# Low parts of U's chunks by adding DMA, beside the top-k and beside the dense weights

## The chip, the cores and the metric

One core of a Trainium2 chip runs the kernel. The metric is the device time of one execution in microseconds (us), taken as the median of several runs. Engines are named as the profile names them: PE (TensorE), DVE (VectorE), ACT (ScalarE), POOL (GpSimd), SP (SyncE, which only issues DMAs here).

## What is computed

The layer is a decoder block of two sub-layers on 512 tokens of width 1024. The part that the change touches is the second one, a retrieval over 16384 single-neuron experts (`peer_u` and `peer_v`, 16384 x 1024 each), 8 heads, 16 experts per head:

```python
q1, q2 = q[..., :PEER_HALF], q[..., PEER_HALF:]
s1 = jnp.einsum('thd,hkd->thk', q1, sub_k1)
s2 = jnp.einsum('thd,hkd->thk', q2, sub_k2)
v1, i1 = lax.top_k(s1, PEER_TOPK)
v2, i2 = lax.top_k(s2, PEER_TOPK)
cand = (v1[..., :, None] + v2[..., None, :]).reshape(-1, PEER_HEADS, PEER_TOPK * PEER_TOPK)
sc, ci = lax.top_k(cand, PEER_TOPK)
e = (jnp.take_along_axis(i1, ci // PEER_TOPK, axis=-1) * PEER_NKEYS
     + jnp.take_along_axis(i2, ci % PEER_TOPK, axis=-1))
g = jax.nn.softmax(sc, axis=-1)
act = jax.nn.gelu(jnp.einsum('thkd,td->thk', peer_u[e], xb), approximate=False)
return jnp.einsum('thk,thkd->td', (g * act), peer_v[e])
```

## The kernel before

Three of the four tiles of 128 tokens go the dense way: every expert's activation is computed for all 384 tokens, multiplied by a dense matrix of weights G (zero where the expert was not chosen), and summed. The fourth tile (DENSE = 3) gathers its 128 chosen rows of `peer_u` and `peer_v` per token, with one indirect DMA of 512 KB per place.

The experts come in 128 chunks of 128. A chunk of U costs 24 matmuls (8 slices of the contraction, each as high x high, high x low, low x high in `mm3`), a chunk of V 18 sets of the same kind. `load_split2` makes the two parts of every such chunk: SP loads `raw` (four buffers), ACT copies it to `hi` in the rounded type (three buffers), and `lo = raw - hi` is made by POOL where `last["pool"]` holds, else by DVE (three buffers).

The order of the stages in the written program:

- *Queries and top-k*: 16 query halves (`query`, `scores`), each a `load_split2`; then chunks of U (U2 and on; U0 and U1 are made earlier) fill PE while DVE works through the top-k of each head (`topk`), which is queued in `bg`. `pump(us)` emits as much of that queue as the planned costs behind each `yield` allow: 5.5 us per query half, then `UPUMP + 1.2` = 2.3 us per chunk of U while POOL makes the low parts. These chunks' activations are spilled to HBM (`Ad`).
- *Dense weights* (`spread`): after `end_topk`, for each of 24 groups of 16 tokens DVE makes one-hot matrices, PE multiplies them (32 products of 128 columns), ACT evicts, and the result goes to HBM (`Gd`). 5 us of it (`GPUMP`) are emitted per chunk of U; 21 of these chunks (`U_resident`, NRES) keep their activations in SBUF. DVE makes the low parts here. `end_spread` ends it, and `VDLY` = 3 more chunks of U follow.
- *V for the resident chunks*, then U and V in alternation for the remaining chunks, then V for the spilled ones. `gather` is emitted among these; four of its gathers need no buffer to come free, and the first eight are tied by `behind` to stand after `last["pool_lo"]`, the last low part that went through POOL.

Softmax's exponential is tied behind the third high part that follows it (`EXPD`). `finish` closes a tile of tokens with a scratch buffer `fin`. The order on each engine's queue is the scheduler's, which may move an instruction ahead of another where no dependency or `behind` forbids it.

Of the kernel before, what the change touches and what calls it, by code (L numbers as in the profile page):

```python
# [8 lines left out]
F32 = mybir.dt.float32  # L9
F32R = mybir.dt.float32r  # L10
# [3 lines left out]
AF = mybir.ActivationFunctionType  # L14
ALU = mybir.AluOpType
AX = mybir.AxisListType

P = 128
D = 1024
S = 512  # L20
NK = D // P
# [7 lines left out]

NTAIL = 4  # L30
FPOOL = {0: 2, 1: 2, 2: 0, DENSE: 0}
UPUMP = 1.1
GUV = 2.9
GU = 0
NPRE = 2
# [19 lines left out]
def block_kernel(ctx, tc, I, out):  # L55
    nc = tc.nc
    PS = bass.MemoryType.PSUM

    def mm3(ps, pairs):
        n = len(pairs)  # L60
        for i, (l, r) in enumerate(pairs):
            nc.tensor.matmul(ps, l.hi, r.hi, start=(i == 0), stop=False)  # L62
            nc.tensor.matmul(ps, l.hi, r.lo, start=False, stop=False)  # L63
            last = nc.tensor.matmul(ps, l.lo, r.hi, start=False, stop=(i == n - 1))  # L64
        return last
# [28 lines left out]
    def ln_stats(pool, src, nm):  # L94
        st = pool.tile([P, 2, 6], F32, name=f"st{nm}", tag="lnst", bufs=2)
        for hh in range(2):
            nc.vector.bn_stats(st[:, hh, :], src[:, hh * 512:(hh + 1) * 512])
        mv = pool.tile([P, 2], F32, name=f"mv{nm}", tag="lnmv", bufs=2)
        nc.vector.bn_aggr(mv, st)
        rs = pool.tile([P, 1], F32, name=f"rs{nm}", tag="lnrs", bufs=2)  # L100
        nc.scalar.activation(rs, mv[:, 1:2], AF.Sqrt, bias=eps)
        nc.vector.reciprocal(rs, rs)
        return mv, rs
# [5 lines left out]
    with ExitStack() as fr:  # L109
# [183 lines left out]
        for n in range(NT):  # L293
            for gh in range(4):
# [4 lines left out]
                if u % 2 == 1:  # L299
                    t = (u % 8) // 2  # L300
# [16 lines left out]
        for j in range(NK):  # L317
            ps = proj_T(load_split(I["w_u"][j], f"u{j}"), hT, f"psu{j}")
            nc.scalar.activation(uT[:, j, :], ps, AF.Gelu)
            if j % 2 == 0:  # L320
                t = j // 2
# [76 lines left out]
        for hh in range(2):  # L398
            for t in range(NT):
# [13 lines left out]
                for kh in range(2):  # L413
# [5 lines left out]
                    for k4 in range(4):  # L419
                        k = 4 * kh + k4  # L420
                        if k < NEV:
                            nc.scalar.activation(hf[:, k4, :], pt[:, k4 * P:(k4 + 1) * P], AF.Identity,
                                                 scale=G2c[:, k:k + 1], bias=B2c[:, k:k + 1])
# [7 lines left out]
    pw = ctx.enter_context(tc.tile_pool(name="pw", bufs=1, reuse_waits="tile"))  # L431
    actp = ctx.enter_context(tc.tile_pool(name="actp", bufs=1, reuse_waits="tile"))
    gat = ctx.enter_context(tc.tile_pool(name="gat", bufs=1, reuse_waits="tile"))
    pu = ctx.enter_context(tc.tile_pool(name="pu", bufs=1, space=PS, reuse_waits="tile"))
    last = {}

    def behind(ins, other):

        tc.add_manual_dep(ins.ins, other.ins.name,
                          mybir.DependencyInfo(mybir.DependencyClass.NoSync, mybir.DependencyReason.DATA))  # L440
# [4 lines left out]
    def load_split2(src, nm, pool=None):  # L445
        raw = pw.tile([P, NK * P], F32, name=f"raw{nm}", tag="raw", bufs=4)
        last["dma"] = nc.sync.dma_start(raw, src)
        hi = (pool or pw).tile([P, NK * P], F32R, name=f"hi{nm}", tag="hi", bufs=1 if pool else 3)
        lo = (pool or pw).tile([P, NK * P], F32R, name=f"lo{nm}", tag="lo", bufs=1 if pool else 3)
        h = nc.scalar.activation(hi, raw, AF.Copy)  # L450
        if "expn" in last:
            last["expn"] -= 1
            if last["expn"] == 0:
                behind(last["exp"], h)
        if last.get("pool"):
            last["pool_lo"] = nc.gpsimd.tensor_sub(lo, raw, hi.bitcast(F32))  # L456
        else:
            last["dve"] = nc.vector.tensor_sub(lo, raw, hi.bitcast(F32))  # L458
        return Split(hi, lo)
# [11 lines left out]
    def pump(us):  # L471
        credit[0] += us
        while credit[0] > 0 and bg:
            try:
                credit[0] -= next(bg[0])
            except StopIteration:
                bg.pop(0)
# [38 lines left out]
    def query(h, half):  # L516
        nm = f"{h}_{half}"
        w = load_split2(I["w_pq"][2 * h + half], f"pq{nm}")
        ps = pu.tile([P, S], F32, name=f"psq{nm}", tag="mm", bufs=2)
        wv = Split(w.hi.rearrange("p (k c) -> p k c", k=NK), w.lo.rearrange("p (k c) -> p k c", k=NK))  # L520
        mm3(ps, [(wv[:, k, :], h2T[:, k, :]) for k in range(NK)])
        qt = tp.tile([P, S], F32, name=f"qt{nm}", tag="qt", bufs=2)
        nc.scalar.copy(qt, ps)
        return qt

    def scores(h, half, qt):
        pss = pq.tile([P, NT, P], F32, name=f"pssc{h}_{half}", tag="s", bufs=2)
        for t in range(NT):
            nc.tensor.matmul(pss[:, t, :], qt[:, t * P:(t + 1) * P], subk[:, half, h, :], start=True, stop=True)
        nc.scalar.copy(sall[:, 2 * h + half, :, :], pss)  # L530
# [67 lines left out]
    def topk_head(h):  # L598
        return topk(f"h{h}_", DENSE, lambda half, j: sall[:, 2 * h + half, j, :],
                    lambda a: a[:, 0:DENSE, 16 * h:16 * h + 16])  # L600
# [92 lines left out]
    def U_resident(i):  # L693

        w = load_split2(I["uT"][i], f"U{i}")
        ps = pu.tile([P, SD], F32, name=f"psU{i}", tag="mm", bufs=2)
        wv = Split(w.hi.rearrange("p (k c) -> p k c", k=NK), w.lo.rearrange("p (k c) -> p k c", k=NK))
        last["U"] = mm3(ps, [(wv[:, k, :], h2T[:, k, 0:SD]) for k in range(NK)])
        slot, n = res["tile"][:, len(res["ids"]), :], res["spread"]
        if n < SD:  # L700
            nc.scalar.activation(slot[:, n:], ps[:, n:], AF.Gelu)
        if n:
            a = actp.tile([P, SD], F32, name=f"act{i}", tag="act", bufs=4)
            nc.scalar.activation(a[:, 0:n], ps[:, 0:n], AF.Gelu)
            nc.vector.tensor_mul(slot[:, 0:n], slot[:, 0:n], a[:, 0:n])
        res["ids"].append(i)

    def U_chunk(i, keep_act):
        w = load_split2(I["uT"][i], f"U{i}")
        ps = pu.tile([P, SD], F32, name=f"psU{i}", tag="mm", bufs=2)  # L710
        wv = Split(w.hi.rearrange("p (k c) -> p k c", k=NK), w.lo.rearrange("p (k c) -> p k c", k=NK))
        last["U"] = mm3(ps, [(wv[:, k, :], h2T[:, k, 0:SD]) for k in range(NK)])
        a = actp.tile([P, SD], F32, name=f"act{i}", tag="act", bufs=4)
        nc.scalar.activation(a, ps, AF.Gelu)
        if not keep_act:
            nc.scalar.dma_start(Ad[i], a)
        return a

    def finish(t, halves):
        vp, rows = vs["lp"], vs["rows"]  # L720
        z = xhat[:, t, :]
        tmp = vp.tile([P, D], F32, name=f"fin{t}", tag="fin", bufs=1)
        for hh in range(2):
            hs = slice(hh * 512, (hh + 1) * 512)
            nc.vector.tensor_mul(tmp[:, hs], halves[hh], rows[0][:, hs])
            nc.vector.scalar_tensor_tensor(z[:, hs], z[:, hs], ALPHA, tmp[:, hs], op0=ALU.mult, op1=ALU.add)
        mv, rs = ln_stats(vp, z, f"o{t}")
        if FPOOL[t]:
            nmu = vp.tile([P, 1], F32, name=f"nmu{t}", tag="nmu", bufs=2)
            nc.scalar.activation(nmu, mv[:, 0:1], AF.Copy, scale=-1.0)  # L730
        for hh in range(2):
            hs = slice(hh * 512, (hh + 1) * 512)
            if hh < 2 - FPOOL[t]:
                nc.vector.scalar_tensor_tensor(z[:, hs], z[:, hs], mv[:, 0:1], rows[1][:, hs], op0=ALU.subtract,
                                               op1=ALU.mult)
                nc.vector.scalar_tensor_tensor(z[:, hs], z[:, hs], rs, rows[2][:, hs], op0=ALU.mult, op1=ALU.add)
            else:
                nc.scalar.activation(z[:, hs], z[:, hs], AF.Identity, bias=nmu)
                nc.gpsimd.tensor_mul(z[:, hs], z[:, hs], rows[1][:, hs])
                nc.scalar.activation(z[:, hs], z[:, hs], AF.Copy, scale=rs)  # L740
                nc.gpsimd.tensor_add(z[:, hs], z[:, hs], rows[2][:, hs])
            nc.sync.dma_start(out[t * P:(t + 1) * P, hs], z[:, hs])
# [61 lines left out]
    bg.append(rows_h2())  # L804
    qt = query(0, 0)
    for j in range(16):
        nxt = query((j + 1) // 2, (j + 1) % 2) if j < 15 else U_chunk(NPRE, False)
        scores(j // 2, j % 2, qt)
        qt = nxt
        if j % 2 == 1:  # L810
            bg.append(topk_head(j // 2))
        pump(QPUMP)
# [16 lines left out]

    def end_spread():  # L830
        done.append(1)
        last["pool"] = False
        return
        yield

    bg += [topk_last(), softmax(), end_topk(), spread(), end_spread()]
    gt = gather()
    n_g = 0
# [19 lines left out]
    while not done or len(res["ids"]) < NRES:  # L858
# [4 lines left out]
        else:  # L863
            U_chunk(i, False)
            spilled.append(i)
            pump(GPUMP if res else UPUMP + 1.2 * bool(last.get("pool")))
        i += 1
# [32 lines left out]
    for run in runs(spilled):  # L900
        load_G(run)
        for j in run:
            if (j - run[0]) % 4 == 0:
                n = min(4, run[-1] + 1 - j)
# [8 lines left out]
    for t in range(DENSE):  # L913
        for n in range(2):
            for m, (wsp, w) in enumerate(tail):
                V_products(t, n, wsp, w, False, m == NTAIL - 1)
        finish(t, vs["acc"][t])
# [61 lines left out]
```

## Time and profile before

| | |
|---|---|
| median of 3 runs | 1722.47 us (1721.66 to 1728.24) |
| the profiled execution | 1727.59 us, span 1725.9 us |
| busy, share of the span | PE 97%, weight loads 84%, DVE 78%, ACT 40%, POOL 28% |
| chain that ended last | PE 55%, DVE 18%, DMA 5% |
| mean granted TensorE clock | 0.991 |

One execution is profiled, and its times are counted from the span's start. Matmuls are pipelined, so the time of one matmul overlaps the next; the distance between two starts is the one that counts. "Idle before" is the time that an engine stood before an instruction, with what released it. The span's stages, by when their instructions run: queries and top-k about 475 to 718 us, dense weights 718 to 886, V of the resident chunks to 985, U and V in alternation to about 1535, V of the spilled chunks to the end.

### The profile page before, as it was taken

The numbers are of one execution on the slowest core, as the hardware profiler recorded it, in microseconds if no ns is written. First come the engines' busy times: TensorE is split into PE (matmuls) and PEld (weight loads), VectorE is DVE, ScalarE is ACT, GpSimd is POOL, SyncE is SP. The second block draws the span as 40 slices with busy tenths as digits, with TensorE's granted clock in tenths as the row PEclk, the third lists the DMA queues.
The fourth block names the chain that finished last, engine by engine and source line by source line (L and its number), as shares of the span: only waits on it lengthen the run. The fifth ranks groups of instructions, "written<-read, shape, count | busy, mean of one in ns | idle before, by whom it ended". The sixth has DMA issues, their size and how long they took to land.

```text
span 1725.9 us, 23559 instructions
## 1 busy us (share of the span) xinstructions
PE 1668.0 (97%) x8658; PEld 1442.8 (84%) x8658; DVE 1353.8 (78%) x2509; ACT 685.9 (40%) x1095; POOL 481.5 (28%) x334
## 2 busy tenths in 40 slices
PE   6999999999999999899999999999999999989997
PEld 3765777788788999899998789999999999978886
DVE  6467786454589999999978888778787888878787
ACT  3467632233343333355543233333333333333333
POOL 2000000000043455400014444444454545531202
PEclk9999999999999999999999999999999999999999
DMA  7602257642252355556699999999899999899982
GB/s 269 201 1 74 98 196 245 219 146 86 77 189 78 103 173 172 191 206 224 211 321 365 363 325 340 320 338 351 312 337 324 326 345 324 311 351 316 305 282 86
DMA packets 162071, 409.92 MB, mean 238 GB/s; under 512 B 22337, under 2 KB 69473, under 8 KB 161698
## 3 DMA queue, kind: packets, MB, share of 16 engines
q1 hardware_dynamic: 112178, 245.35, 42.3%
q0 software_dynamic: 36960, 134.50, 21.6%
q10 hardware_dynamic: 12816, 28.55, 4.3%
q8 instruction: 68, 1.11, 0.3%
q14 instruction: 49, 0.40, 0.1%
HBM read 377.07 MB, written 31.01 MB: 236 GB/s over the span
## 4 chain that ended last, share of the span: by engine, by line
PE 55%; DVE 18%; DMA 5%; issue 4%; POOL 2%; ACT 0%; SPq 0%; DVEq 0%; POOLq 0%; ACTq 0%
PE acc L801 8%; PE acc L800 8%; PE acc L797 8%; PE psU L64 7%; PE psU L62 6%; PE psU L63 6%; DMA wa<-in_w_ada_dram 2%; POOL ru L667 2%; DMA ru<-in_peer_u_dram,idx 1%; DMA rawV<-in_peer_v_dram 1%; PE pso L63 1%; PE pso L64 1%; PE psga L64 1%; PE psga L62 1%; PE pspa L64 1%
## 5 line engine op out<-in xcount | busy, mean ns | idle before, releaser
L64 PE MATMUL psU<-h2Thi,loU 128*128 128x384 f32 x1008 | 340.6, 338 | 5.4 <-DVE loU L458 5.3
L62 PE MATMUL psU<-h2Thi,hiU 128*128 128x384 f32 x1008 | 340.8, 338 | 0.0
L63 PE MATMUL psU<-h2Tlo,hiU 128*128 128x384 f32 x1008 | 339.3, 337 | 0.0
L797 PE MATMUL acc<-hiV,wh 128*128 128x512 f32 x768 | 300.1, 391 | 4.5 <-ACT wh L782 4.5
L800 PE MATMUL acc<-loV,wh 128*128 128x512 f32 x768 | 301.5, 393 | 1.5 <-DVE loV L458 1.5
L801 PE MATMUL acc<-hiV,wl 128*128 128x512 f32 x768 | 301.1, 392 | 0.3 <-DVE wl L783 0.3
L667 POOL DMA_INDIRECT ru<-in_peer_u_dram,idx x128 | 159.0, 1242 | 360.6 <-DVE ru L671 341.2
L680 POOL DMA_INDIRECT rv<-in_peer_v_dram,idx x128 | 176.4, 1378 | 247.9 <-DVE facc L686 226.6
L458 DVE TENSOR_TENSOR loV<-rawV,hiV 128x1024 fp32r<-128x1024 f32 x128 | 156.4, 1222 | 101.2 <-ACT hiV L450 100.9
L450 ACT ACTIVATE hiV<-rawV 128x1024 fp32r<-128x1024 f32 x128 | 135.1, 1055 | 224.2 <-PE psU L63 184.1
L450 ACT ACTIVATE hiU<-rawU 128x1024 fp32r<-128x1024 f32 x126 | 134.0, 1063 | 194.5 <-PE psU L63 105.5
L64 PEld LDWEIGHTS psU<-h2Thi,loU 128*128 128x128 f32 x1008 | 190.4, 189 | 7.7 <-DVE loU L458 7.6
L63 PEld LDWEIGHTS psU<-h2Tlo,hiU 128*128 128x128 f32 x1008 | 190.6, 189 | 2.6
L62 PEld LDWEIGHTS psU<-h2Thi,hiU 128*128 128x128 f32 x1008 | 190.4, 189 | 2.6
L797 PEld LDWEIGHTS acc<-hiV,wh 128*128 128x128 f32 x768 | 144.9, 189 | 33.7 <-ACT wh L782 5.1
L671 DVE SCALAR_TENSOR_TENSOR ru<-ru,h2n 128x1024 f32<-128x1024 f32 x128 | 154.4, 1221 | 22.0 <-DMA ru<-in_peer_u_dram,idx 21.8
L800 PEld LDWEIGHTS acc<-loV,wh 128*128 128x128 f32 x768 | 144.8, 189 | 32.0 <-DVE loV L458 3.1
L801 PEld LDWEIGHTS acc<-hiV,wl 128*128 128x128 f32 x768 | 144.8, 189 | 31.1 <-DVE wl L783 0.7
L686 DVE SCALAR_TENSOR_TENSOR facc<-rv,wg,facc 128x1024 f32<-128x1024 f32 x126 | 159.4, 1278 | 11.7 <-DMA rv<-in_peer_v_dram,idx 11.7
L456 POOL TENSOR_TENSOR lopq<-rawpq,hipq 128x1024 fp32r<-128x1024 f32 x16 | 40.7, 2544 | 325.1 <-ACT hipq L450 325.1
L782 ACT ACTIVATE wh<-wf 128x384 fp32r<-128x384 f32 x107 | 56.2, 526 | 183.4 <-DVE wf L778 100.5
L458 DVE TENSOR_TENSOR loU<-rawU,hiU 128x1024 fp32r<-128x1024 f32 x95 | 115.7, 1218 | 1.4 <-ACT hiU L450 1.4
(628 smaller groups left out, 2942.4 us busy)
## 6 DMA issues: line engine op xcount, KB each, us to landing
rawU<-in_uT_dram SPq DMA_DIRECT2D x128, 512.0 KB
rawV<-in_peer_v_dram SPq DMA_DIRECT2D x128, 512.0 KB
wa<-in_w_ada_dram SPq DMA_DIRECT2D x48, 512.0 KB
G<-Gd SPq DMA_DIRECT2D x11, 1536.0 KB
Gd<-stg ACTq DMA_DIRECT2D x24, 592.0 KB
rawpq<-in_w_pq_dram SPq DMA_DIRECT2D x16, 512.0 KB
Ad<-act ACTq DMA_DIRECT2D x38, 192.0 KB
ar<-Ad SPq DMA_DIRECT2D x9, 768.0 KB
```

The costliest lines, as they stand in the source:

```text
L62: nc.tensor.matmul(ps, l.hi, r.hi, start=(i == 0), stop=False)
L63: nc.tensor.matmul(ps, l.hi, r.lo, start=False, stop=False)
L64: last = nc.tensor.matmul(ps, l.lo, r.hi, start=False, stop=(i == n - 1))
L450: h = nc.scalar.activation(hi, raw, AF.Copy)
L458: last["dve"] = nc.vector.tensor_sub(lo, raw, hi.bitcast(F32))
L667: d = nc.gpsimd.indirect_dma_start(out=rows, out_offset=None, in_=I["peer_u"], in_offset=bass.IndirectOffsetOnAxis(ap=idx[:, s:s + 1], axi ...
L671: paced(nc.vector.scalar_tensor_tensor(rows, rows, 1.0, h2n, op0=ALU.mult, op1=ALU.mult, accum_out=wg[:, s:s + 1]))
L680: nc.gpsimd.indirect_dma_start(out=rows, out_offset=None, in_=I["peer_v"], in_offset=bass.IndirectOffsetOnAxis(ap=idx[:, s:s + 1], axis=0))
L686: paced(nc.vector.scalar_tensor_tensor(fa, rows, wg[:, s:s + 1], fa, op0=ALU.mult, op1=ALU.add))
L797: m = nc.tensor.matmul(acc, l.hi, r.hi, start=st, stop=False)
L800: nc.tensor.matmul(acc, l.hi, r.lo, start=False, stop=False)
L801: nc.tensor.matmul(acc, l.lo, r.hi, start=False, stop=sp_)
```

## The change

The low part of every second load from the 17th on (the first chunk of U in `load_split2` is the 17th load) is made without DVE or POOL arithmetic while `last["dma_lo"]` holds, which is from that chunk to the end of the dense weights: ACT writes the negated high part into `lo`, and a DMA issued from POOL adds `raw` to it. The other loads go as before. `lo` has four buffers instead of three. The scratch of `finish` moves into the buffers of the gathered rows. `UPUMP` goes from 1.1 to 1.35.

```diff
-UPUMP = 1.1
+UPUMP = 1.35
...
-        lo = (pool or pw).tile([P, NK * P], F32R, name=f"lo{nm}", tag="lo", bufs=1 if pool else 3)
+        lo = (pool or pw).tile([P, NK * P], F32R, name=f"lo{nm}", tag="lo", bufs=1 if pool else 4)
         h = nc.scalar.activation(hi, raw, AF.Copy)
...
-        if last.get("pool"):
+        last["n"] = last.get("n", 0) + 1
+        if last.get("dma_lo") and last["n"] % 2:
+            nc.scalar.activation(lo, hi.bitcast(F32), AF.Copy, scale=-1.0)
+            last["pool_lo"] = nc.gpsimd.dma_start(lo.bitcast(F32), raw, accum_op=ALU.add)
+        elif last.get("pool"):
             last["pool_lo"] = nc.gpsimd.tensor_sub(lo, raw, hi.bitcast(F32))
         else:
             last["dve"] = nc.vector.tensor_sub(lo, raw, hi.bitcast(F32))
...
-        tmp = vp.tile([P, D], F32, name=f"fin{t}", tag="fin", bufs=1)
+        tmp = gat.tile([P, D], F32, name=f"fin{t}", tag="rows", bufs=4)
...
     for j in range(16):
+        last["dma_lo"] = j == 15
         nxt = query((j + 1) // 2, (j + 1) % 2) if j < 15 else U_chunk(NPRE, False)
...
     def end_spread():
         done.append(1)
-        last["pool"] = False
+        last["pool"] = last["dma_lo"] = False
```

## Rows read from the trace of the kernel before

**Rows 1.** Windows by stage: engines' busy time (instructions), granted clock, DMA share, GB/s.

```profile
576.00:718.00 142.00, 142.00 (x815) 140.11 (x814) 141.62 (x592) 50.34 (x71) 76.42 (x31) 1.00 0.47 157
718.00:729.00 11.00, 6.63 (x27) 5.98 (x26) 10.79 (x16) 3.48 (x5) 5.87 (x4) 0.69 0.61 211
729.00:886.00 157.00, 153.83 (x1379) 147.89 (x1379) 149.46 (x183) 86.81 (x170) 0.00 (x0) 1.00 0.64 227
886.00:985.00 99.00, 97.52 (x443) 81.63 (x442) 79.97 (x119) 34.47 (x47) 47.22 (x38) 1.00 1.00 363
```

**Rows 2.** Timeline of PE beside the dense weights: start, us, instruction.

```profile
809.85 0.24 PE L643 MATMUL psg<-oh,oh 128*128 128x128 f16 x1
...
811.65 0.22 PE L644 MATMUL psg<-oh,oh 128*128 128x128 f16 x1
...
812.29 0.33 PE L62 MATMUL psU<-h2Thi,hiU 128*128 128x384 f32 x1
...
814.89 0.33 PE L62 MATMUL psU<-h2Thi,hiU 128*128 128x384 f32 x1
```

**Rows 3.** Timeline of PE at the hand-over; brackets: idle before, releaser.

```profile
721.04 0.45 PE L64 MATMUL psU<-h2Thi,loU 128*128 128x384 f32 x1 [2.05 <-DVE loU L458]
...
723.98 0.45 PE L615 MATMUL ptg<-ident,gs 128*128 128x128 f32 x1 [2.32 <-DVE gs L595]
...
724.54 0.52 PE L64 MATMUL psU<-h2Thi,loU 128*128 128x384 f32 x1
...
728.64 0.33 PE L62 MATMUL psU<-h2Thi,hiU 128*128 128x384 f32 x1
```

**Rows 4.** Waits from 715 to 886 us: total, times, longest.

```profile
PEld psU L64 <- DVE loU L458: 4.5, 8, 2.4
```

**Rows 5.** Timeline of POOL beside the top-k.

```profile
619.62 2.40 POOL L456 TENSOR_TENSOR loU<-rawU,hiU 128x1024 fp32r<-128x1024 f32 x1 [1.75 <-ACT hiU L450]
623.78 2.50 POOL L456 TENSOR_TENSOR loU<-rawU,hiU 128x1024 fp32r<-128x1024 f32 x1 [1.76 <-ACT hiU L450]
```

**Rows 6.** Timeline of DVE beside the top-k.

```profile
582.38 2.40 DVE L581 TENSOR_TENSOR ohlh__4260<-ohlh__4260 128x96 f16<-128x96 f16 x1
...
623.94 2.56 DVE L581 TENSOR_TENSOR ohlh__4630<-ohlh__4630 128x384 f16<-128x384 f16 x1
...
627.46 0.35 DVE L581 TENSOR_TENSOR ohlh__4639<-ohlh__4639 128x384 f16<-128x384 f16 x1
...
707.55 2.49 DVE L568 SCALAR_TENSOR_TENSOR ab1l__5824<-ab1l__5824,posl__5637 128x128 f16<-128x128 f16 x1
```

**Rows 7.** The tile loU: instructions, ns shortest/median/longest, first and last start.

```profile
L458 DVE TENSOR_TENSOR loU<-rawU,hiU x95: 1209/1219/1225, 719.8 to 1528.4; 128x1024 fp32r<-128x1024 f32 x95
L456 POOL TENSOR_TENSOR loU<-rawU,hiU x31: 2401/2408/2927, 575.9 to 707.0; 128x1024 fp32r<-128x1024 f32 x31
```

**Rows 8.** The tile ru (gathered rows) from 886 to 985 us.

```profile
L671 DVE SCALAR_TENSOR_TENSOR ru<-ru,h2n x38: 1215/1220/1228, 889.4 to 981.4; 128x1024 f32<-128x1024 f32 x38
...
L667 POOL DMA_INDIRECT ru<-in_peer_u_dram,idx x38: 936/1014/1781, 890.9 to 982.9; - x38
```

**Rows 9.** Timeline of ACT beside the top-k.

```profile
701.68 1.06 ACT L450 ACTIVATE hiU<-rawU 128x1024 fp32r<-128x1024 f32 x1 [2.72 <-PE psU L63]
702.65 0.47 ACT L714 ACTIVATE act<-psU 128x384 f32<-128x384 f32 x1
703.15 0.33 ACTq L716 DMA_DIRECT2D Ad<-act  x1
```

**Rows 10.** Timeline of POOL early on: two copies of 128 KB within SBUF.

```profile
58.94 0.76 POOL L206 DMA_DIRECT2D kd<-kd  x1 [24.52 <-ACT kd L204]
```

**Rows 11.** DMA from 60.2 to 62.2 us, in 40 slices: busy tenths; queue's packets, MB, share.

```profile
DMA  0939374893930000089699449989000000000000
...
q0 software_dynamic: 96, 0.26, 59.8%
```

**Rows 12.** DMA from 718 to 735 us: the software queue, four gathers.

```profile
q0 software_dynamic: 576, 2.10, 32.4%
```

## The prediction

> **What bounds the kernel now.** I read the windows by stage first. Beside the top-k (576 to 718 us) PE and DVE are both busy all the time, 142.0 and 141.6 of 142 us, with the DMA engines at 0.47. In the 11 us after it PE is busy 6.6 and its granted clock is 0.69. Beside the making of the dense weights (729 to 886) DVE is busy 149.5 of 157 us, and from 886 to 985 the DMA engines stand at 1.00 [rows 1]. So the reader is to look for TensorE time that is lost, and that "busy" hides since matmuls overlap: by start-to-start times an instruction of U costs 0.173 us (812.29 to 814.89 holds 15 steps) and one of the weights' products 0.058 us (809.85 to 811.65 holds 31) [rows 2]. A chunk of U is 24 x 0.173 = 4.16 us.
>
> Then the PE timeline at the hand-over from top-k to weights. PE stands 2.05 us for the low part of a chunk, which DVE has yet to make, and 2.32 us for the softmaxed gates. Behind these gaps the clock is at the lower of its two levels, 1.2 GHz: 724.54 to 728.64 takes 4.1 us for 13 steps [rows 3] that cost 2.25 at 2.4 GHz, so 1.85 are lost. Together 2.05 + 2.32 + 1.85 = 6.2 us.
>
> In the stage of the weights 729 to 886 holds 1379 matmuls [rows 1]: 768 products, some 6 transposes, and so about 605 of U. 768 x 0.058 + 605 x 0.173 + 1.5 = 150.8 us, and 157 pass: 6.2 us are lost. Of waits that end at DVE, PE's weight loads for a low part show 4.5 us [rows 4]. After that stage nothing that the change touches has slack to give: what can be won is 6.2 + 6.2 = 12.4 us.
>
> **Part 1, the top-k's DVE.** A subtraction on POOL takes 2.4 us, one every 4.16 us [rows 5]. While one runs, some DVE instructions stand until it ends: a 128x384 sum takes 0.35 us beside none, and 2.56 us when it starts at 623.94, within the subtraction of 623.78 to 626.28 [rows 5, 6]. Between 576 and 710 I count 15 DVE instructions stretched by over 1.5 us, the first at 582.38, the last at 707.55 [rows 6], 2.13 us each on average: 32 us, beside 31 subtractions [rows 7]. The change lets the 17th load and every second one after it go by DMA (load 17 is U2, so all even chunks). UPUMP raises the credit per chunk from 2.3 to 2.55. Before, 30 chunks (U3 to U32) pay 69 us of planned DVE work; 69 / 2.55 asks for 27, U3 to U29. With U2 that is 14 subtractions and 14 adding DMAs. In proportion the stretches fall to 32 x 14/31 = 14.5 us, so DVE ends its top-k 17.5 us sooner; PE comes to the hand-over 3 x 4.16 = 12.5 us sooner. DVE was the late one and gains 5 us on PE. From both sides: every subtraction left catches one instruction (14 x 2.13 = 30, DVE gains 2 us and is 10 us late), or none does (32 gained). I take the proportion, since about half of 31 were caught, and say that of the 6.2 us at the hand-over 0.7 remain: **-5.5 us**.
>
> Does POOL hold DVE as well when it issues a DMA? Beside 38 gathers no DVE product of two SBUF inputs took over 1.228 us, at a median of 1.220 [rows 8]. No.
>
> **Part 2, the weights' DVE.** The stage holds 25 chunks by its credits (24 groups of 5.1 and 3 of 0.4, over 5 a chunk), U30 to U54; 13 are even. Each spares DVE one 1.22 us subtraction [rows 7]: 149.5 - 13 x 1.22 = 133.6 us of DVE beside 150.8 of PE. DVE then has a tenth of slack where it now runs at PE's own pace; groups still come in lumps, so I recover 5 of the 6.2 us (between 0 and 6.2): **-5.0 us**.
>
> **Part 3, the path of an adding DMA.** This is new: two copies on ACT in a row, an issue on POOL, a transfer from SBUF to SBUF that also reads its target. ACT starts a high part when PE frees the buffer of three chunks earlier, so the low part must stand two chunks and two matmuls later, 2 x 4.16 + 0.35 = 8.67 us. ACT takes a high part at 701.68, the gelu at 702.65, the store's issue until 703.48 [rows 9]; the negated copy behind these ends 2.86 us after the start, ahead of them 2.0. From a POOL issue at 58.94 to its first data, 60.25, pass 1.31 us [rows 10, 11]. The two small copies kept the engines 0.598 x 2.0 = 1.2 us for 0.26 MB, 0.6 us for 128 KB, 2.4 for 512 KB [rows 11]. Four gathers from HBM kept them 0.324 x 17 = 5.5 us for 2.1 MB, 1.38 each [rows 12]. So 2.0 + 1.31 + 1.38 = 4.7 us from below. From above the target's reading doubles 2.4 to 4.8, half the engines' time is taken already (4.8 / 0.53 = 9.1), and an issue takes 1.78 us as the slowest gather's does, not 0.76 [rows 8, 10]: 2.86 + 1.31 + 1.0 + 9.1 = 14.3. The nearest row is the small copy, alone or sharing the engines (2.4 to 4.5): 6.6 to 8.7 us, against 8.67. It just fits: **0**, the thinnest cover of this forecast. Beside the weights a chunk takes 157/25 = 6.3 us, the lead is over 12 us, and the cover is better. Engines: 0.47 + 2.4/8.32 = 0.76 of their time, with 4.8 it would be 1.05.
>
> ACT gains 27 copies of about 1.06 us [rows 9]; it is busy 50.3 of 142 us beside the top-k and 86.8 of 157 beside the weights [rows 1]: 0. On POOL an issue waits for its negated copy; the subtraction behind it needs a high part that comes 4.16 us later, so nothing is held up. A raw buffer is now kept until the DMA lands, some 3 to 5 us longer than by POOL; with four of them the next load still has about 4 us to spare: 0. The first gathers are tied behind the last low part that POOL handles, so four of them move from 720 to the stage's end: 4 x 1.38 = 5.5 us of DMA time out of a stretch with 0.64 into one that runs into the full stage from 886 [rows 1, 12]. Some 20 us remain there at 0.8 or less: 0, at worst +5.5. The three chunks that are kept instead of spilled cost PE the same, and spare three stores and loads: 0. The fourth low buffer frees nothing that the three high ones don't hold: 0. The closing sums' scratch in the gather's buffers: same engine, long free, 0.
>
> A rule of the Trainium skill speaks against the change (SBUF — State Buffer, section "SBUF: two separate sides", its box on DMAs issued by GpSimd): while DVE runs an instruction in a two-port mode GpSimd can't write descriptors, and the DMA seems stalled. The gathers' issues, 0.94 to 1.78 us [rows 8], agree with a hold of up to 0.8 us. By the short issue the cover stands as above; by a hold each time the upper value, 8.7, becomes 9.5 us, 0.4 us of waiting in each of 14 chunks, and the sum 6 us worse.
>
> **Sum.** -5.5 - 5.0 = -10.5 us on the profiled 1727.6 (span 1725.9) gives 1717.1; that execution is 5.1 us over the median of 1722.5, so against the median 1712.0.
>
> **Rivals.** (a) *The adding DMA lands late beside the top-k: slower.* If the path takes L over 8.67 us, PE waits in every second chunk; a wait gives the next one as much more lead, so (L - 8.67)/2 each, 14 times. At L = 10.2 that eats all 10.5 us; at 11.5 it is 14 x 1.4 = 20, and with one gap over 2 us and the lower clock behind it as at the hand-over (1.85) 1712 + 22 = 1734. For it: the shared engines, the doubled read, issues that vary by 0.8 us. Against it: the lone copies' rate. Chance 0.21. (b) *The relief is real but PE was nearly full: same.* The 6.2 us of the weights' stage come from the order of ACT and PE rather than DVE, or DVE meets PE late at the hand-over since the fewer subtractions catch more: then 2 to 4 us remain, 1720, between 1715 and 1727. For it: only 4.5 us of waits there name DVE's low parts [rows 4]. Chance 0.20. (c) *The change does not do what it says*, that is, POOL's issue holds DVE like a subtraction: so that DVE saves little, meets PE late after 3 chunks fewer, and only the weights' 5 us less the longer wait at the hand-over (2 to 5 us) remain: 1720. Rows 8 speak against it. Chance 0.04.
>
> **How the numbers follow.** The forecast has 0.55, with 1706 to 1718 as its own range. Under it, (b), (c) and the nearer half of (a), 1705 to 1734 leaves out some 0.15, chiefly landings so late that PE waits longer than priced. About 0.5%, 8.6 us, is what a measurement of this kernel tells from no change. 1713.9 lies in my own range, and I put three quarters of it below: 0.41 faster. The rest of it, (b), (c) and landings that just eat the gain make 0.40 within 0.5%; 0.19 are slower.
>
> **What would show it.** Right: matmuls of U stay 0.173 us apart beside the top-k; fewer than 9 stretched DVE instructions there; no gap over 1 us and the full clock at the hand-over; DVE's idle time in the weights' stage rises to 15 us or more. Wrong: PE gaps at the third matmul of even chunks, released by the DMA queue; DVE's i2s later than PE's last chunk; raw loads late because buffers are held; gathers late after the weights.

## The result, and the profile after

The changed kernel takes 1746.3 us (median of 4 runs, 1744.9 to 1747.4) where the kernel before, beside it, takes 1722.07. The ratio of the means, 1.0132, has a 95% interval of 1.0113 to 1.0150; differences in us are of medians. The kernel is slower by 24 us. The forecast was 1712.0 us, and its range ended at 1734. The profiled execution took 1746.12 us, with a span of 1743.9. One later execution of the kernel before took 2374 us at a granted clock of 0.655 and is left out of every median here.

The same four stages as in [rows 1], now of the changed kernel:

```profile
576.00:718.00 142.00, 139.25 (x799) 135.15 (x798) 128.90 (x588) 65.80 (x88) 46.81 (x29) 1.00 0.76 212
718.00:729.00 11.00, 11.00 (x113) 10.68 (x111) 10.68 (x15) 6.38 (x13) 0.87 (x1) 1.00 0.92 274
729.00:886.00 157.00, 135.36 (x1190) 129.55 (x1188) 123.00 (x154) 86.55 (x162) 13.96 (x14) 0.94 0.74 233
886.00:985.00 99.00, 97.30 (x441) 81.50 (x440) 77.45 (x115) 34.85 (x48) 45.08 (x35) 0.99 1.00 355
```

The reader is to see two changes of opposite sign. At the hand-over (718 to 729) PE went from 6.63 busy us of 11 at a clock of 0.69 to 11.00 at 1.00: the forecast's first gain is there. Beside the dense weights (729 to 886) PE went from 153.83 busy us to 135.36, and the mean clock from 1.00 to 0.94: 18.5 us of new idle time. The lower clock adds some 5.3 in the three windows shown further down (5.00 x 0.45 + 4.24 x 0.49 + 2.41 x 0.42), and the idle time beside the top-k 2.75; the hand-over gives back 4.4 of idle time and the 1.85 of [rows 3]. The sum is +20.3, beside 18.5 between the two profiled executions: by it, the stage of the weights is the whole loss. (The medians lie 24.2 apart, since the profiled execution of the kernel before is 5.5 us over its median.)

What PE waits for there, from 715 to 900 us (total, times, longest):

```profile
POOL loU L458 <- ACT loU L457: 136.8, 10, 24.3
ACT res L705 <- PE psU L64: 36.7, 14, 8.9
PEld psU L64 <- DMA loU<-rawU: 22.7, 7, 7.0
PE psU L64 <- DMA loU<-rawU: 20.6, 7, 6.7
```

PE stands 20.6 us for the adding DMA (the line of the weight loads is the same wait seen from their own queue). POOL, in its turn, waits for the negated copy on ACT; nothing on POOL holds an issue up. The three longest waits in PE's timeline (start, duration, instruction, in brackets the idle time before it):

```profile
749.18 0.69 PE L64 MATMUL psU<-h2Thi,loU 128*128 128x384 f32 x1 [3.50 <-DMA loU<-rawU]
...
763.45 0.42 PE L62 MATMUL psU<-h2Thi,hiU 128*128 128x384 f32 x1
763.71 0.34 PE L63 MATMUL psU<-h2Tlo,hiU 128*128 128x384 f32 x1
770.76 0.69 PE L64 MATMUL psU<-h2Thi,loU 128*128 128x384 f32 x1 [6.71 <-DMA loU<-rawU]
...
882.59 0.69 PE L64 MATMUL psU<-h2Thi,loU 128*128 128x384 f32 x1 [6.42 <-DMA loU<-rawU]
```

These are U36, U38 and U54 (U with a number is that chunk of U). Behind each the clock is at its lower level (5-us windows; PE's busy time stands first, the clock third from the end):

```profile
750.00:755.00 5.00, 5.00 (x18) 5.00 (x18) 2.91 (x3) 0.00 (x0) 0.00 (x0) 0.55 0.66 214
...
770.00:775.00 5.00, 4.24 (x13) 4.24 (x14) 3.89 (x4) 0.00 (x0) 0.00 (x0) 0.51 0.95 217
...
880.00:885.00 5.00, 2.41 (x8) 2.41 (x9) 1.71 (x2) 1.06 (x1) 2.92 (x2) 0.58 0.99 281
```

Why U38 is so late stands in ACT's timeline, and POOL's issue behind it:

```profile
756.22 2.07 ACT L649 ACTIVATE stg<-psg 128x512 f32<-128x512 f32 x4
758.14 1.08 ACT L450 ACTIVATE hiU<-rawU 128x1024 fp32r<-128x1024 f32 x1
...
761.82 0.40 ACT L705 ACTIVATE res<-psU 128x272 f32<-128x272 f32 x1 [2.59 <-DMA Gd<-stg]
762.11 0.26 ACT L708 ACTIVATE act<-psU 128x112 f32<-128x112 f32 x1
762.30 2.07 ACT L649 ACTIVATE stg<-psg 128x512 f32<-128x512 f32 x4
764.22 1.08 ACT L457 ACTIVATE loU<-hiU 128x1024 fp32r<-128x1024 f32 x1
```
```profile
765.59 0.87 POOL L458 DMA_DIRECT2D loU<-rawU  x1 [24.27 <-ACT loU L457]
```

The high part of U38 is made at 758.14. The negated copy does not follow it: between them stand the gelu of the chunk just before (761.82, when U37's last matmul has ended at 761.78) and four evictions of products that PE makes right up to the chunk's start. It starts at 764.22, and the DMA is issued at 765.59, when PE has been in the chunk since 763.45. Before the change DVE's subtraction needed only the high part, so this order on ACT cost nothing.

The DMA itself, over the whole run (shortest, median, longest; first and last start; in the last line from issue to landing, the arrival of its data):

```profile
L462 DVE TENSOR_TENSOR loU<-rawU,hiU x85: 1211/1220/1227, 703.0 to 1559.0; 128x1024 fp32r<-128x1024 f32 x85
L457 ACT ACTIVATE loU<-hiU x27: 1048/1052/1104, 573.0 to 874.5; 128x1024 fp32r<-128x1024 f32 x27
L458 POOL DMA_DIRECT2D loU<-rawU x27: 869/875/954, 574.7 to 875.9; - x27
L460 POOL TENSOR_TENSOR loU<-rawU,hiU x14: 2388/2392/2491, 578.6 to 693.5; 128x1024 fp32r<-128x1024 f32 x14
...
DMA to landing us min/median/max: 4.6/6.0/8.7
```

### The profile page after: what moved, and what is told of

It reads as the page before. It is cut to its first block, busy times and chain, and to the rows that moved or that the text cites. A ratio compares the mean times of both kernels' runs of the same rounds, so it can differ in the third digit from the quotient of the medians.

```text
span 1743.9 us, 23617 instructions
## 1 busy us (share of the span) xinstructions
PE 1671.5 (96%) x8658; PEld 1443.8 (83%) x8658; DVE 1317.9 (76%) x2499; ACT 712.1 (41%) x1122; POOL 470.1 (27%) x344
## 4 chain that ended last, share of the span: by engine, by line
PE 65%; issue 9%; DMA 6%; POOL 2%; DVE 1%; ACT 1%; DVEq 0%; POOLq 0%; SPq 0%
PE psU L64 9%; PE psU L62 8%; PE psU L63 8%; PE acc L804 8%; PE acc L805 8%; PE acc L801 8%; DMA loU<-rawU 3%; POOL ru L671 2%; DMA wa<-in_w_ada_dram 2%; PE psq L62 2%; PE psq L64 2%; PE psq L63 2%; PE pso L62 1%; PE psga L64 1%; PE pso L63 1%
## 5 line engine op out<-in xcount | busy, mean ns | idle before, releaser
L684 POOL DMA_INDIRECT rv<-in_peer_v_dram,idx x128 | 183.6, 1434 | 234.1 <-DVE facc L690 213.1
L675 DVE SCALAR_TENSOR_TENSOR ru<-ru,h2n 128x1024 f32<-128x1024 f32 x128 | 154.1, 1221 | 18.5 <-DMA ru<-in_peer_u_dram,idx 18.4
L462 DVE TENSOR_TENSOR loU<-rawU,hiU 128x1024 fp32r<-128x1024 f32 x85 | 103.7, 1220 | 18.0 <-ACT hiU L450 18.0
```

What stands on the lines that cost most here:

```text
L675: paced(nc.vector.scalar_tensor_tensor(rows, rows, 1.0, h2n, op0=ALU.mult, op1=ALU.mult, accum_out=wg[:, s:s + 1]))
L684: nc.gpsimd.indirect_dma_start(out=rows, out_offset=None, in_=I["peer_v"], in_offset=bass.IndirectOffsetOnAxis(ap=idx[:, s:s + 1], axis=0))
```

## Experiments

Theory A: beside the weights the order of ACT's queue decides. The negated copy stands behind work that waits for PE's last results, so the DMA starts too late for its chunk. Theory B: the transfer is too slow. Theory C: the longer budget UPUMP unbalances the stage. "Idle" is 157 us less PE's busy time in 729 to 886 us, and the waits are those of PE for the adding DMA from 715 to 900 us, both of each kernel's profiled execution; the time is the median against the kernel before in the same comparison. A profiled execution can lie some us from the median; where a reading hangs on that, it is said.

| kernel | idle | clock | waits: us (times, longest) | time, us |
|---|---|---|---|---|
| before | 3.2 | 1.00 | none | 0 |
| changed | 21.6 | 0.94 | 20.6 (7, 6.7) | +24.2 |
| top-k half, budget 1.35 | 2.8 | 1.00 | none | -7.7 |
| top-k half, budget 1.1 | 3.4 | 1.00 | none | -1.9 |
| weights half, budget 1.1 | 10.7 | 0.99 | 6.3 (6, 2.0) | +9.5 |
| changed, budget 1.1 | 14.3 | 0.99 | 10.0 (5, 3.6) | +10.5 |
| changed, plain copy | 14.9 | 0.93 | 12.0 (3, 5.4) | +11.8 |
| changed, copy ahead of one chunk's work | 12.2 | 0.98 | 10.6 (7, 3.6) | +15.3 |
| changed, copy ahead of two chunks' gelus | 18.4 | 0.97 | 10.7 (4, 4.3) | +21.1 |
| changed, negated part first | 10.5 | 0.97 | 0.3 (1, 0.3) | +5.4 |
| changed, copy ahead of all of two chunks' work | 3.0 | 0.99 | 0.6 (1, 0.6) | -0.7 |

### Each half alone

```diff
         tk.close()
+        last["dma_lo"] = False
         last["pool"] = PLO > 1
```

> The changed kernel, but the adding DMA ends with the top-k; beside the dense weights DVE subtracts again, as before. Theory A (beside the weights ACT's queue holds the negated copy behind the gelu and the evictions of the chunk before, so the DMA starts too late for its chunk): the 32.6 us that PE lost between 725 and 900 us go back to about 10 and the gain at the hand-over (about 5 us) stays: 1714 to 1720 us. Theory B (the adding transfer is too slow at 6 us from issue to landing, wherever it stands): PE still waits beside the top-k, so 1719 to 1724. Theory C (the larger budget UPUMP of 1.35, which pulls the top-k forward, unbalances the weights stage): 1738 or more, since the budget stays.

1716.44 us, a ratio of 0.9957 (0.9941 to 0.9974): faster than both kernels. Two windows of it:

```profile
718.00:729.00 11.00, 10.75 (x104) 10.27 (x104) 11.00 (x16) 6.01 (x13) 0.00 (x0) 1.00 0.61 218
729.00:886.00 157.00, 154.21 (x1304) 146.99 (x1304) 146.66 (x184) 84.83 (x164) 6.57 (x6) 1.00 0.71 249
```

The gain at the hand-over stays and the loss in the weights' stage is gone. The adding DMA beside the top-k is all but in time (PE waits 0.8 us for it in all) with the same transfer, which speaks against B there, and the budget alone does no harm, which speaks against C in its plain form.

```diff
-UPUMP = 1.35
+UPUMP = 1.1
...
     for j in range(16):
-        last["dma_lo"] = j == 15
...
         tk.close()
+        last["dma_lo"] = True
```

> The other half alone: POOL subtracts beside the top-k as before, with the budget UPUMP of before (1.1); every second low part beside the dense weights comes from the adding DMA. Theory A: the loss of the weights stage is all here, 23 us over before: 1738 to 1750 us. Theory B: the same, 1738 to 1750. Theory C (the budget): 1722 to 1727, as the budget is the old one.

1733.58 us, 1.0051 (1.0038 to 1.0064). A loss, as A and B had it, but of 9.5 us, not 14 or more: a miss. The halves add up to +1.8 us where the whole costs +24.2. Something in the whole, then, is more than its parts; the budget is the only thing in which this half differs from the whole's stage of the weights, apart from what came before.

### The budget

```diff
-UPUMP = 1.1
+UPUMP = 1.35
```

in the kernel before, and nothing else:

> The kernel before with the budget UPUMP of 1.35 alone, POOL and DVE subtracting as before. It tells what of the gain of the top-k half (1716.4 against 1724.1) the low parts are needed for. If the gain came from fewer stretched DVE operations, DVE cannot keep the shorter plan here: PE runs out at the hand-over by more than before, 1724 to 1732 us. If it came from the budget alone: 1714 to 1719.

1726.89 us, 1.0018 (1.0004 to 1.0032). PE reaches the hand-over sooner, and DVE does not:

```profile
716.18 0.69 PE L64 MATMUL psU<-h2Thi,loU 128*128 128x384 f32 x1 [11.77 <-DVE loU L458]
719.12 0.45 PE L615 MATMUL ptg<-ident,gs 128*128 128x128 f32 x1 [1.93 <-DVE gs L595]
```

The 2.05 us of [rows 3] became 11.77: three chunks fewer are 12.5 us, and PE only stands for them. Without the spared subtractions the budget buys nothing.

The top-k half with the old budget:

```diff
-UPUMP = 1.35
+UPUMP = 1.1
...
         tk.close()
+        last["dma_lo"] = False
```

> The adding DMA beside the top-k alone, with the old budget (1.1). DVE is spared half of POOL's subtractions but is given no more work per chunk. If the hand-over was lost to a DVE that ran behind, DVE is now on time and the two gaps of 2 us before 725 us go, but three more chunks lie ahead of the hand-over than with 1.35 and none is needed: 1716 to 1722. If the gain needs both, 1722 to 1726.

1721.98 us, 0.9995 (0.9978 to 1.0012). Its profile shows what DVE is spared, since the stretch from 576 to 718 us holds the same 592 DVE instructions as before [rows 1]:

```profile
576.00:718.00 142.00, 142.00 (x816) 140.02 (x814) 121.15 (x592) 65.05 (x86) 54.53 (x35) 1.00 0.79 225
718.00:729.00 11.00, 10.83 (x77) 10.40 (x76) 10.18 (x11) 6.04 (x12) 0.00 (x0) 1.00 0.63 244
```

141.62 - 121.15 = 20.5 us of DVE. The two gaps at the hand-over are gone, yet the median says no change: by the medians the gain of the top-k half needs both, the relief and the budget that uses it. The profiled execution took 1717.49 us and is the fastest of ten, so it does not show what the others, up to 1729.28, lost.

The changed kernel with the old budget:

```diff
-UPUMP = 1.35
+UPUMP = 1.1
```

> The changed kernel with the old budget: all adding DMAs stay. The two halves alone cost -7.7 and +9.5 us, together +24. If the missing 22 us come from how the longer budget (1.35) lines the chunks up with the weights' groups, this comes near the sum of the halves: 1724 to 1732. If they come from having adding DMAs in both stages, it stays at 1738 to 1748.

1734.30 us, 1.0062 (1.0040 to 1.0084), between the two expected ranges: +10.5 us, nearer the sum of the two halves at this budget (-1.9 + 9.5 = +7.6) than the changed kernel's +24.2. So the adding DMAs of one stage spoil the other little; the other 13.7 us of the changed kernel come with 1.35. The stage and its waits:

```profile
729.00:886.00 157.00, 142.70 (x1277) 136.53 (x1275) 133.61 (x166) 89.40 (x169) 16.59 (x15) 0.99 0.82 258
```
```profile
PE psU L64 <- DMA loU<-rawU: 10.0, 5, 3.6
```

The same DMA beside the weights, as often (12 times), but no wait over 3.6 us, and a clock below 1.00 only from 870 to 880 us. The budget shifts by three chunks which chunk meets which group of weights, and with that the order of ACT's queue. C is right only in this sense: the budget decides how bad A gets.

### The transfer

```diff
-            last["pool_lo"] = nc.gpsimd.dma_start(lo.bitcast(F32), raw, accum_op=ALU.add)
+            last["pool_lo"] = nc.gpsimd.dma_start(lo.bitcast(F32), raw)
```

> The changed kernel with the addition taken out of the DMA: it is issued at the same place, but copies raw over lo and reads nothing of lo, so the subtraction is left out and the low part is the raw weight. Theory A (the order on ACT): the transfer begins as late as before and PE waits nearly as long: 1736 to 1746 us. Theory B (the addition makes the transfer slow): landing falls from 6 to under 4 us and the time to 1722 to 1732.

1735.92 us, 1.0079 (1.0054 to 1.0104), between the two expectations. The order on ACT is that of the changed kernel, U38's issue comes 7.45 us after its high part in both, and PE then has its low part 3.8 us after the issue instead of 5.2 (U54: 4.5 instead of 6.7). So the addition costs 1.4 to 2.2 us on the path and takes part of the blame, some 12 of 24 us by the medians (the six executions spread from 1731.80 to 1743.74), since it lengthens each wait. PE still waits 5.4 us at the longest. This does not settle A against B; the order does.

### The order on ACT

```diff
-            nc.scalar.activation(lo, hi.bitcast(F32), AF.Copy, scale=-1.0)
+            neg = nc.scalar.activation(lo, hi.bitcast(F32), AF.Copy, scale=-1.0)
             last["pool_lo"] = nc.gpsimd.dma_start(lo.bitcast(F32), raw, accum_op=ALU.add)
+            for g in last.get("acts", []):
+                behind(g, neg)
```

where `acts` holds the gelus and evictions written since the load before.

> The changed kernel with one thing added: on ACT's queue the negated copy is tied ahead of the gelus and the evictions that were written between the load before and this one. The same DMAs and the same copies run, only earlier. Theory A: the waits of 3.5 to 7 us for the adding DMA beside the weights mostly go; what stays is where the high part itself comes late: 1718 to 1730 us. Theory B: PE goes on waiting for a transfer of 6 us: 1738 to 1747.

1739.37 us, 1.0084 (1.0061 to 1.0107): a miss for A, inside the range set for B. But the two waits of over 6 us are gone and the total is halved,

```profile
PE psU L64 <- DMA loU<-rawU: 10.6, 7, 3.6
```

but one chunk's work is not enough: U36, for one, stands behind the work of the chunk two before it, and PE has only 6.3 us to do after that.

```diff
+        neg = None
+        if last.get("dma_lo") and last["n"] % 2:
+            neg = nc.scalar.activation(lo, raw, AF.Copy, scale=-1.0)
         h = nc.scalar.activation(hi, raw, AF.Copy)
+        if neg is not None:
+            behind(h, neg)
...
-            nc.scalar.activation(lo, hi.bitcast(F32), AF.Copy, scale=-1.0)
```

> The changed kernel, but ACT writes the negated part straight from raw and ahead of the high part, so the adding DMA can start up to a chunk sooner in both stages. It is the same number of copies and DMAs. Theory A (lead, not transfer: in the changed kernel the DMA of U38 and U54 is issued 2.2 us after PE has begun the chunk, that of U48 0.5 us before it): with the lead a chunk longer PE's waits for the DMA beside the weights nearly vanish, and of the 32.6 us lost between 725 and 900 us about 12 to 16 stay: 1722 to 1732 us. Theory B (shared DMA engines or the transfer itself): waits of 2 to 7 us stay, 1740 to 1748.

1729.22 us, 1.0022 (1.0005 to 1.0039). The transfer takes no less (issue to landing 4.6, 6.2 and 8.3 us at the least, median and most beside the weights, where the changed kernel has 4.6, 5.4 and 8.7), and PE no longer waits for it:

```profile
PEld psU L62 <- ACT hiU L454: 5.7, 3, 3.1
PE psU L62 <- ACT hiU L454: 4.9, 3, 2.8
...
PE psU L64 <- DMA loU<-rawU: 0.3, 1, 0.3
```

As the whole account B falls with this. Now the high part, pushed behind the negated one, comes late three times.

As a measure of the order, take PE's work, at the pitches of [rows 2], from the last result of PE that ACT must take in ahead of the negated copy, to the chunk's first low product (its first matmul that reads the low part). In the changed kernel this lead and the wait at the low product are, in us: U38 0.3 and 6.71, U54 2.2 and 6.42, U48 5.0 and 1.73 (behind 1.23 for its high part), U36 6.3 and 3.50, U52 6.3 and 1.05, U46 6.3 and 0.63; 8.7 or more, and none above 0.6, for the other chunks beside the weights. The order is not the whole of it: U36, U46 and U52 have the same lead, and U36 waits longer since its DMA took 8.7 us to land, theirs 5.1 and 5.5. With the old budget (1.1) no lead is under 4 us. The next kernel gives all of them a long lead:

```diff
...
+            for g in last.get("acts0", []) + last.get("acts", []):
+                behind(g, neg)
...
+        last["acts0"], last["acts"] = last.get("acts", []), []
         return Split(hi, lo)
```

> The changed kernel, with every gelu and eviction written in the two loads before tied behind the negated copy on ACT's queue. As a measure, lead: PE's work, in its queue's order at pitches of 0.173 and 0.058 us, between the last result of PE that ACT must take in before the negated copy and the chunk's first low product. In the changed kernel it is 0.3 us for U38, 2.2 for U54, 5.0 for U48, 6.3 for U36, U46 and U52, over 8.7 for the rest; here it is at least 11 us for all chunks beside the weights. Theory A (the wait is the chain from that result, some 1.3 to 2 us of ACT, 0.9 of issue and 5.4 of landing, less the lead): no wait for the DMA is left there, and 1716 to 1728 us, if later gelus and evictions cost PE nothing. Theory B (the transfer is slow because of what runs beside it): waits of 2 us and more stay: 1735 to 1745.

1721.70 us, 0.9991 (0.9975 to 1.0006): all 24 us against the kernel before are back, with the same 27 copies and DMAs. Against the top-k half (-7.7) some 7 us are missing.

```profile
729.00:886.00 157.00, 154.02 (x1324) 147.35 (x1323) 134.69 (x170) 97.22 (x177) 19.02 (x18) 0.99 0.89 288
```
```profile
PE psU L64 <- DMA loU<-rawU: 0.6, 1, 0.6
```

ACT now takes the negated copy of U38 (752.10) ahead of the gelu and the evictions; the next chunk's high part stands before it:

```profile
751.13 1.06 ACT L450 ACTIVATE hiU<-rawU 128x1024 fp32r<-128x1024 f32 x1 [0.70 <-PE psU L63]
752.10 1.04 ACT L457 ACTIVATE loU<-hiU 128x1024 fp32r<-128x1024 f32 x1
753.05 0.39 ACT L709 ACTIVATE res<-psU 128x288 f32<-128x288 f32 x1
753.47 2.06 ACT L653 ACTIVATE stg<-psg 128x512 f32<-128x512 f32 x4
```

The window from 729 to 886 us is not quite the stage, which starts and ends at other times in each kernel. From the first to the last product of the weights pass, in the kernel before, the changed kernel (U54's wait falls behind its last product), the top-k half with budget 1.35 and this one:

```profile
735.40:882.20 146.80, 143.63 (x1321) 137.82 (x1320) 141.34 (x175) 82.17 (x163) 0.00 (x0) 1.00 0.63 223
717.40:876.20 158.80, 143.55 (x1296) 137.41 (x1295) 131.32 (x165) 88.87 (x168) 9.02 (x11) 0.96 0.73 233
715.40:861.90 146.50, 143.45 (x1320) 137.84 (x1320) 144.54 (x178) 82.17 (x163) 0.00 (x0) 1.00 0.63 221
719.30:862.40 143.10, 142.34 (x1319) 137.35 (x1319) 131.63 (x166) 91.40 (x170) 14.28 (x15) 1.00 0.87 276
```

With the long lead the stage itself is 3.4 us shorter than without adding DMAs in it. The profiled execution (1725.03 us, the slowest of ten) loses more around it than that. Beside the one of the top-k half (1714.37 us) its stage starts 3.9 us later, from the last product to the first matmul of V pass 16.7 us instead of 12.2, and the rest takes 4.3 us longer. In the 16.7 us an eviction waits for a store to HBM, and a high part behind it comes late:

```profile
865.09 0.60 ACT L653 ACTIVATE stg<-psg 128x512 f32<-128x512 f32 x1 [4.06 <-DMA Gd<-stg]
...
868.15 0.44 PE L62 MATMUL psU<-h2Thi,hiU 128*128 128x384 f32 x1 [1.57 <-ACT hiU L450]
```

One thing that differs there is that the first four gathers, tied behind the last low part on POOL, are issued from 848.35 us instead of 696.13, into DMA engines that stand at 1.04 and 0.99 from 850 to 855 and 855 to 860 us (0.81 and 0.76 in the top-k half). That they delay the store is not shown: no run moves them alone, and with budget 1.1 they move as far (from 708.7 to 868.6) while the time from the last product to the end stays (841.0 us in the top-k half, 841.5 with all adding DMAs).

With only the gelus of these two chunks tied (kept with their chunk's number in `gelu`), not the evictions:

```diff
...
+            for c, g in last.get("gelu", []):
+                if c >= int(nm[1:]) - 2:
+                    behind(g, neg)
```

> The changed kernel with only the gelus of the two chunks before tied behind the negated copy; the evictions of the weights stay ahead of it. Lead by the same measure: still 0.3 us for U38 (an eviction holds it), 5.0 for U48, 6.3 for U36 and U52, but 7.8 for U54 and 12.3 for U46. Theory A: U38 still waits 6 to 7 us, U48 and U36 some 3.5, U54 under 1.5: 8 to 10 us less wait than in the changed kernel, 1734 to 1740. If the gelus were what matters, no wait is left: 1716 to 1728.

1743.47 us, 1.0129 (1.0104 to 1.0155): a miss by the median. The profiled execution, 1737.57 us, is the fastest of four (the others took 1743.04 to 1746.05). In it the waits for the DMA fell by 10 us and the time by 8.6 beside the changed kernel's profiled execution, as A expected; what the other three lost no profile shows. In this one PE also waits for high parts, and ACT for the products of the weights:

```profile
ACT stg L652 <- PE psg L651: 29.3, 9, 7.1
...
PE psU L64 <- DMA loU<-rawU: 10.7, 4, 4.3
PE psU L62 <- ACT hiU L450: 5.1, 3, 3.5
```

So the gelus are not what matters alone: U38 still waits 4.3 us behind an eviction. This is consistent with A. That the tie must cover all that waits for PE is shown by the kernel before this one, not by this one's median.

### A better version

The top-k half with the negated part first:

```diff
+        if last.get("dma_lo") and last["n"] % 2:
+            neg = nc.scalar.activation(lo, raw, AF.Copy, scale=-1.0)
         h = nc.scalar.activation(hi, raw, AF.Copy)
+        if neg is not None:
+            behind(h, neg)
...
         tk.close()
+        last["dma_lo"] = False
```

> The adding DMA beside the top-k alone (budget 1.35), with the negated part written straight from raw, ahead of the high part, so that the DMA has a chunk's time more. Only 2.4 us were lost between 575 and 725 us in the top-k half, so there is little to win: 1713 to 1717. If the earlier copy holds the high part up, 1718 to 1722.

1714.84 us, 0.9958 (0.9944 to 0.9973): faster than the kernel before by 7.6 us, and so than the changed one by some 32. It cannot be told from the top-k half without it (1716.44).

The top-k half with a still longer budget:

```diff
-UPUMP = 1.35
+UPUMP = 1.6
...
         tk.close()
+        last["dma_lo"] = False
```

> The adding DMA beside the top-k alone, with a budget UPUMP of 1.6 instead of 1.35. DVE was busy 54 of 60 us from 640 to 700 us in the top-k half with 1.35, so a tenth of it is still free. If DVE keeps the plan, the top-k ends a chunk or two sooner, worth little more: 1713 to 1718. If not, PE runs out at the hand-over, as the kernel before with 1.35 did (one gap of 11.9 us at 704): 1720 to 1728.

1722.23 us, 0.9993 (0.9979 to 1.0008). The hand-over held (PE busy 11.00 us of 11 from 718 to 729), so DVE kept the plan; what was lost again is spread over the stages behind it. Its longest waits of PE beyond those of the top-k half, 2.03 us for a one-hot matrix at 839.50 (1.40 there) and 2.08 for ACT at 974.57, do not add up to it. Left open.

## Why the prediction was wrong

**The failed step** is in part 3: "Beside the weights a chunk takes 157/25 = 6.3 us, the lead is over 12 us, and the cover is better". The lead was worked out from the buffers, as beside the top-k. There it holds: in the changed kernel a DMA is issued 2.68 us after the start of its high part in nearly every chunk, and the low product follows 8.6 us or little more after that start. Beside the weights ACT has the gelus and the evictions in its queue as well, in an order fixed before the run. The negated copy started up to 8.9 us after the high part (U48), and U38's high part itself only 5.3 us ahead of its chunk. The prediction read ACT's rows beside the top-k [rows 9] and took the weights' stage for an easier case of the same; no row of ACT's timeline in that stage entered it. The runs show it: with the same DMAs and a long lead PE's waits for them there go from 20.6 to 0.6 us and the time from +24.2 to -0.7 us.

**Rival (a)** had the mechanism (a late landing, a wait at the low product, the lower clock behind the long ones) and a price, 1734, that is 12 us short, but put it beside the top-k. There PE's waits for the DMA are 2.6 us in all.

**Part 1** was right: -5.5 us were expected, and the top-k half gives -7.7. DVE was spared 20.5 us, against 17.5. The stretches fell further than in proportion: by a count of instructions that take 1.5 us more than the median of their form, 13 before, 2 in the changed kernel and 1 in the top-k half, where under 9 were forecast. The one gap left at the hand-over is 0.56 us. That budget and relief are worth something only together was part of the argument and is confirmed by the medians of both single runs.

**Part 2** was right for the stage and not for the whole. With the long lead DVE's load fell as reckoned (134.7 us from 729 to 886, 133.6 forecast). From the first to the last product PE's idle time is 0.8 us where it was 3.2 before and 3.1 in the top-k half, and the stage is 3.7 and 3.4 us shorter, of the 5.0 that were forecast. The top-k half's two longest waits there, 0.94 and 1.40 us for one-hot matrices from DVE, are gone; how much of this is owed to ACT's new order no run separates. It did not reach the whole: that kernel is some 7 us behind the top-k half, by what lies before and behind the stage. Of the terms put at 0, the moved gathers (at worst +5.5) may be part of that. Rival (b), that this stage has little to give, is thus not what was seen inside it.

**The rest of part 3.** From the high part's start to the landing 6.6 to 8.7 us were estimated; beside the top-k it is 2.68 + 6.3 = 9.0 by the medians (issue to landing 5.0, 6.3 and 7.1 us at the least, median and most), so the thin cover was a little too thin: 2.6 us of waits, not 0. POOL's issue takes 0.869 to 0.954 us in all 27 cases. The Trainium skill (SBUF — State Buffer, section "SBUF: two separate sides") says that DVE, while it runs an instruction in a two-port mode, keeps GpSimd from writing descriptors. In these issues no hold is seen, and whether some of the spread from issue to landing is one, no run here shows.

**Rival (c)** does not hold: DVE was relieved in full.

## What to carry to other kernels

A step that moves to another engine inherits that engine's queue: before counting buffers as the lead, read the queue of the new engine in the very stage, and find the last thing ahead of the step that waits for the bottleneck. A transfer in the path of each chunk asks for that lead by construction, with its copies tied ahead of all work that waits for the engine it feeds. And where a change covers two stages, time each alone, since a real gain in one was hidden here by a loss four times as large in the other.

## What was not expected of the hardware

An adding DMA of 512 KB within SBUF, issued from POOL, takes 0.87 us to issue and 4.6 to 8.7 us to land; as a plain copy it is issued in 0.54 to 0.57 us, and in the two chunks compared PE has its data 1.4 and 2.2 us sooner. Fourteen subtractions of 2.4 us on POOL stretched two DVE instructions by over 1.5 us in the changed kernel and one in the top-k half, where 31 had stretched 13; why so few was not tried. In the changed kernel PE's three waits of 3.5 us and more were followed by 5-us windows at a mean clock of 0.51 to 0.58; its waits of under 2 us were not. With the gelus alone tied, a wait of 3.63 us (U36) was not either: the clock stayed at 1.00 until 763 us. Beside the top-k, with the same instructions there, PE lost 0.8 us to the DMA in the top-k half alone and 3.5 us in the kernel with the long lead, and the latter ends 5 to 7 us later, by the medians or by each one's distance from the kernel before; this stays open.
